# Inverting the triangular blocks of an RWKV-7 mixer on GpSimd instead of VectorE

## The chip, the cores and the metric

The kernel runs on one core of one Trainium2 chip. The metric is the device time of one execution in microseconds (us). Three runs of the kernel before took 2212.31, 2216.68 and 2216.26 us, median 2216.26 us.

## The reference

Two blocks follow each other on 256 tokens of width 2048. The second one has two mixers side by side, RWKV-7 (16 heads of 64 channels) and an attention with low-rank projections (MLA), then a projection and a feed-forward part. The change lies in the RWKV-7 mixer, whose core is a recurrence over tokens for each head:

```python
def rwkv7_scan(r, w, k, v, a, b):
    def step(state, inp):
        r_t, w_t, k_t, v_t, a_t, b_t = inp
        sa = jnp.einsum('bhvk,bhk->bhv', state, a_t)
        state = (state * w_t[:, :, None, :]
                 + sa[..., None] * b_t[:, :, None, :]
                 + v_t[..., None] * k_t[:, :, None, :])
        return state, jnp.einsum('bhvk,bhk->bhv', state, r_t)
    ...
```

The kernel doesn't step over tokens. It takes chunks of 64 tokens, and inside a chunk the term `sa` needs the inverse of a unit triangular 64x64 matrix. Of that matrix the kernel inverts the two 32x32 blocks on the diagonal by substitution and gets the rest with small matmuls.

## The kernel before, in words

Nearly all of the time goes into float32 matrix products whose weights are streamed from memory once. SP loads a piece of weights (`wraw`, 128 partitions x 1024 numbers). In `wsplit` ScalarE (ACT) casts it to a rounded half `whi` (L285), and VectorE (DVE) makes the rest, `wlo` = `wraw` - `whi` (L286). TensorE (PE) then needs both: in `lin` 24 matmuls for each piece at L327 to L329, two with `whi` and one with `wlo` for each product. `whi` and `wlo` have three buffers each, so ACT can be at most three pieces ahead of PE.

There are three phases. In phase b, `mixers` runs four groups G of four heads. For each group `rkv_lin` makes k, r and v (three large products), stores them with POOL's DMAs (`kdr`, L926), and `rwkv_prepare` loads them back (L938), forms the decays, and calls `tri_inverse` (L1044 on). `rwkv_chunks` then uses the inverse; it is called one group later, so that the group's chain of small steps runs beside the large products of the next groups and of the MLA part. The chain is long and each step is small: the products that fill PE meanwhile don't depend on it.

`tri_inverse` works as follows. DVE makes `Lc` from the masked blocks (L1051). ACT issues a DMA that stores it as `xd` (L1052) and eight DMAs that load it back (L1057, L1058) as `L`: each of the 32 blocks of a group lies along the free axis in all partitions that work on it. POOL issues the load of an identity into `T` (L1061). Then 31 steps follow, j = 0 to 30, each of two instructions: `tmp = l_j * t_j` (L1066, the tile `Tt` in the profile) and `T = T + tmp` (L1067). Both have 128 partitions and n x m numbers, n = j // 4 + 1, m = 31 - j, so from 8 to 76 numbers and 1560 in all for each line. Each instruction needs the one ahead of it. Last, ACT issues four DMAs that store `T` as `td` (L1069), one that loads it back in another layout as `Tc` (L1071), and DVE transposes `Tc` (L1072). `Lc`, `T` and `tmp` share the tag `tri` with two buffers, and `L` has one, so that one group's inversion must be over before the next one's begins.

Each engine runs its instructions in a fixed order, and so do the DMA issues in the queues of SP, ACT and POOL: an instruction that waits holds up what stands behind it on its engine. The order is made when the kernel is built, by a planner that plays the whole program through with costs of its own and takes, among what is ready, what has the highest priority: `rwkv_prepare` and `rwkv_chunks` are raised by `RP` = 6000, the weight pieces by `HP` = 1200. The planner's order is thus different when an instruction moves to another engine.

Of the kernel before, what the change touches and what calls it, by code (L numbers as in the profile page):

```python
# [12 lines left out]
ALU = mybir.AluOpType  # L13
# [103 lines left out]
class Kern:  # L117
# [926 lines left out]
    def tri_inverse(self, G, AB):  # L1044

        nc = self.nc
        xd = self.dr.tile([32, 32, 32], F32, tag=f"xd{G}", name=self.nm("xd"))
        td = self.dr.tile([32, 8, 4, 32], F32, tag=f"td{G}", name=self.nm("td"))
        small = lambda s, tag="tri": self.wk.tile([128, 8, 32], F32, tag=tag, name=self.nm(s))
        Lc = small("Lc")  # L1050
        nc.vector.tensor_tensor(Lc[:], AB[:, :, 0:32], AB[:, :, 32:64], ALU.add)  # L1051
        nc.scalar.dma_start(xd[:].rearrange("(c q) j i -> (q j) c i", q=4), Lc[:])  # L1052
        L = self.wk.tile([128, 768], F32, tag="L", bufs=1, name=self.nm("L"))
        L0, L1 = L[:, 0:512].rearrange("p (j i) -> p j i", i=32), L[:, 512:768].rearrange("p (j i) -> p j i", i=16)
        for q in range(4):
            qs = slice(32 * q, 32 * q + 32)
            nc.scalar.dma_start(L0[qs], xd[:, 0:16, :])  # L1057
            nc.scalar.dma_start(L1[qs], xd[:, 16:32, 16:32])  # L1058
        T, tmp = small("T"), small("Tt")
        o, n = CB["tinit"]  # L1060
        nc.gpsimd.dma_start(T[:], self.A["c_blk"][:, o : o + n].rearrange("p (c i) -> p c i", c=8))  # L1061
        for j in range(31):
            n, m = j // 4 + 1, 31 - j
            lj = (L0[:, j, j + 1 : 32] if j < 16 else L1[:, j - 16, j - 15 : 16]).unsqueeze(1).to_broadcast([128, n, m])
            tj = T[:, 0:n, j : j + 1].to_broadcast([128, n, m])
            nc.vector.tensor_tensor(tmp[:, 0:n, 0:m], lj, tj, ALU.mult)  # L1066
            nc.vector.tensor_tensor(T[:, 0:n, j + 1 : 32], T[:, 0:n, j + 1 : 32], tmp[:, 0:n, 0:m], ALU.add)  # L1067
        for q in range(4):
            nc.scalar.dma_start(td[:, :, q, :], T[32 * q : 32 * q + 32, :, :])  # L1069
        Tc, Tt = small("Tc", "trc"), small("Ttr", "trc")  # L1070
        nc.scalar.dma_start(Tc[:], td[:].rearrange("(c h) e q i -> (h e q) c i", h=4))  # L1071
        nc.vector.transpose(Tt[:], Tc[:])  # L1072
        return Tc, Tt
# [512 lines left out]
```

## Time and profile before

| what | value |
|---|---|
| median of 3 runs | 2216.26 us |
| the profiled execution: its time, its span | 2216.77 us, 2213.8 us |
| PE busy | 2168.2 us, 98% of the span |
| DVE busy | 1711.1 us, 77% |
| ACT busy | 1207.7 us, 55% |
| POOL busy | 106.4 us, 5% |
| mean granted TensorE clock | 0.995 of full speed |
| DMA traffic | 412.76 MB, mean 186 GB/s |

A busy share counts the time in which an engine has an instruction at work. PE's matmuls overlap each other, so the mean duration of one is longer than the distance between two. A PE that is busy all the time tells that the other engines are hidden behind it, whatever their share. The profile's time from the first to the last instruction is its span; about 3 us lie around it.

### The profile page before, as it was taken

The numbers are of one execution on the slowest core, as the hardware profiler recorded it, in microseconds if no ns is written. First come the engines' busy times: TensorE is split into PE (matmuls) and PEld (weight loads), VectorE is DVE, ScalarE is ACT, GpSimd is POOL, SyncE is SP. The second block draws the span as 40 slices with busy tenths as digits, with TensorE's granted clock in tenths as the row PEclk, the third lists the DMA queues.
The fourth block names the chain that finished last, engine by engine and source line by source line (L and its number), as shares of the span: only waits on it lengthen the run. The fifth ranks groups of instructions, "written<-read, shape, count | busy, mean of one in ns | idle before, by whom it ended". The sixth has DMA issues, their size and how long they took to land.

```text
span 2213.8 us, 36348 instructions
## 1 busy us (share of the span) xinstructions
PE 2168.2 (98%) x13687; PEld 1935.8 (87%) x13687; DVE 1711.1 (77%) x3176; ACT 1207.7 (55%) x1861; POOL 106.4 (5%) x253
## 2 busy tenths in 40 slices
PE   8999999999999999999999999999999999999997
PEld 7899988888899878899999888888888888888887
DVE  6999999778989889787787877776765576556765
ACT  6456636565566546665666556455443444444443
POOL 3100000000000000001100000020000000000000
PEclk9999999999999999999999999999999999999999
DMA  8875556666665457677774435476666666566654
GB/s 238 240 211 164 173 162 209 194 207 189 188 183 170 149 166 219 212 214 216 221 183 123 129 88 158 157 255 203 191 189 192 194 189 190 190 196 188 189 190 140
DMA packets 374511, 412.76 MB, mean 186 GB/s; under 512 B 40456, under 2 KB 327429, under 8 KB 373952
## 3 DMA queue, kind: packets, MB, share of 16 engines
q1 hardware_dynamic: 336464, 366.06, 54.4%
q0 software_dynamic: 10960, 31.79, 4.6%
q10 hardware_dynamic: 26912, 12.60, 2.4%
q8 instruction: 107, 1.75, 0.3%
q14 instruction: 68, 0.56, 0.1%
HBM read 390.47 MB, written 19.92 MB: 185 GB/s over the span
## 4 chain that ended last, share of the span: by engine, by line
PE 91%; DVE 3%; DMA 2%; ACT 2%; issue 1%; ACTq 1%; SPq 0%; DVEq 0%
PE wide L353 35%; PE wide L355 18%; PE lin L328 4%; PE lin L327 4%; PE lin L329 4%; PE lin L1401 3%; PE lin L1402 3%; PE lin L1400 3%; PE dn L1402 2%; PE dn L1401 2%; PE dn L1400 2%; PE po L709 1%; DVE wlo L286 1%; PE lin L1231 1%; PE lin L1232 1%; PE lin L1233 1%
## 5 line engine op out<-in xcount | busy, mean ns | idle before, releaser
L285 ACT CAST whi<-wraw 128x1024 fp32r<-128x1024 f32 (+1 forms) x708 | 725.2, 1027 | 670.6 <-PE wide L353 290.8
L286 DVE TENSOR_TENSOR wlo<-wraw,whi 128x1024 fp32r<-128x1024 f32 (+1 forms) x708 | 843.4, 1192 | 313.6 <-ACT whi L285 307.0
L353 PE MATMUL wide<-xs,whi 128*128 128x512 f32 x3492 | 853.0, 393 | 6.0 <-ACT whi L285 3.7
L353 PEld LDWEIGHTS wide<-xs,whi 128*128 128x128 f32 x3492 | 638.0, 189 | 129.8 <-ACT whi L285 5.3
L355 PEld LDWEIGHTS wide<-xs,wlo 128*128 128x128 f32 x3492 | 454.2, 191 | 25.8 <-DVE wlo L286 5.5
L355 PE MATMUL wide<-xs,wlo 128*128 128x256 f32 x3492 | 466.3, 284 | 3.6 <-DVE wlo L286 3.6
L327 PE MATMUL lin<-xs,whi 128*128 128x256 f32 x844 | 241.1, 286 | 1.2 <-ACT whi L285 0.6
L329 PE MATMUL lin<-xs,wlo 128*128 128x256 f32 x844 | 240.2, 285 | 1.6 <-DVE wlo L286 1.6
L328 PE MATMUL lin<-xs,whi 128*128 128x256 f32 x844 | 240.2, 285 | 0.0
L591 DVE SCALAR_TENSOR_TENSOR cy<-apad,vc_cw,cy 128x256 f32<-128x256 f32 x480 | 229.6, 480 | 6.7
L327 PEld LDWEIGHTS lin<-xs,whi 128*128 128x128 f32 x844 | 161.5, 191 | 2.7 <-ACT whi L285 0.8
L329 PEld LDWEIGHTS lin<-xs,wlo 128*128 128x128 f32 x844 | 161.5, 191 | 2.4 <-DVE wlo L286 1.8
L328 PEld LDWEIGHTS lin<-xs,whi 128*128 128x128 f32 x844 | 161.6, 191 | 1.1 <-issue 0.7
L1401 PE MATMUL lin<-wlo,xs 128*128 128x512 f32 (+1 forms) x304 | 117.4, 386 | 0.5 <-DVE wlo L286 0.5
L1402 PE MATMUL lin<-whi,xs 128*128 128x512 f32 (+1 forms) x304 | 117.0, 385 | 0.0
L1400 PE MATMUL lin<-whi,xs 128*128 128x512 f32 (+1 forms) x304 | 113.7, 386 | 1.2 <-ACT whi L285 1.2
L1400 PEld LDWEIGHTS lin<-whi,xs 128*128 128x128 f32 x304 | 57.1, 188 | 12.8 <-ACT whi L285 1.6
L1401 PEld LDWEIGHTS lin<-wlo,xs 128*128 128x128 f32 x304 | 57.2, 188 | 11.9 <-DVE wlo L286 1.0
L1400 PE MATMUL dn<-whi,xs 128*128 128x512 f32 (+1 forms) x176 | 67.0, 381 | 0.0
L1401 PE MATMUL dn<-wlo,xs 128*128 128x512 f32 (+1 forms) x176 | 67.0, 381 | 0.0
L1402 PE MATMUL dn<-whi,xs 128*128 128x512 f32 (+1 forms) x176 | 67.0, 381 | 0.0
L1402 PEld LDWEIGHTS lin<-whi,xs 128*128 128x128 f32 x304 | 57.1, 188 | 11.1
(544 smaller groups left out, 2401.1 us busy)
## 6 DMA issues: line engine op xcount, KB each, us to landing
wraw<-in_w_in_dram SPq DMA_DIRECT2D x244, 512.0 KB, 4.1
wraw<-in_w_out_dram SPq DMA_DIRECT2D x89, 512.0 KB, 4.0
wraw<-in_ffn_w_gate_dram SPq DMA_DIRECT2D x88, 512.0 KB, 4.1
wraw<-in_ffn_w_up_dram SPq DMA_DIRECT2D x88, 512.0 KB, 3.9
wraw<-in_ffn_w_down_dram SPq DMA_DIRECT2D x87, 512.0 KB, 4.3
wraw<-in_w_pg_dram SPq DMA_DIRECT2D x64, 512.0 KB, 4.5
bt<-btab POOLq DMA_DIRECT2D x32, 192.0 KB, 3.1
btab<-bF ACTq DMA_DIRECT2D x4, 1024.0 KB, 8.1
```

The lines of the kernel that those rows point to most:

```text
L285: nc.scalar.copy(hi[:], src)
L286: self.lo = nc.vector.tensor_tensor(lo[:], src, hi[:].bitcast(F32), ALU.subtract)
L327: nc.tensor.matmul(ps[:, t, :], lhsT=h, rhs=xh_, start=((t, k) == first), stop=False)
L328: nc.tensor.matmul(ps[:, t, :], lhsT=h, rhs=xl_, start=False, stop=False)
L329: nc.tensor.matmul(ps[:, t, :], lhsT=l, rhs=xh_, start=False, stop=((t, k) == last))
L353: nc.tensor.matmul(ps[t][:], lhsT=hi[:, i, ts], rhs=S.both(k).rearrange("p u c -> p (u c)"), **flags)
L355: nc.tensor.matmul(ps[t][:, :SEQ], lhsT=lo[:, i, ts], rhs=S.hi(k), **flags)
L591: prev, tail = tail, nc.vector.scalar_tensor_tensor(y, ap[:, t, k : k + SEQ], cw[:, k : k + 1], y, ALU.mult, ALU.add)
L709: nc.tensor.matmul(po[:, qb, g, :], lhsT=pT[:, kb, qb * 128 : qb * 128 + 128], rhs=vd[:, kb, j, :], start=(kb == 0), stop=(kb == 1))
L1400: nc.tensor.matmul(ps, lhsT=zh, rhs=hi, start=(k == 0), stop=False)
L1401: nc.tensor.matmul(ps, lhsT=zh, rhs=lo, start=False, stop=False)
L1402: nc.tensor.matmul(ps, lhsT=zl, rhs=hi, start=False, stop=(k == nt - 1))
```

## The change

The two instructions of each of the 31 steps are issued on POOL (GpSimd) instead of DVE. There are 4 groups, so 248 instructions move. Nothing else is written differently:

```diff
         for j in range(31):
             n, m = j // 4 + 1, 31 - j
             lj = (L0[:, j, j + 1 : 32] if j < 16 else L1[:, j - 16, j - 15 : 16]).unsqueeze(1).to_broadcast([128, n, m])
             tj = T[:, 0:n, j : j + 1].to_broadcast([128, n, m])
-            nc.vector.tensor_tensor(tmp[:, 0:n, 0:m], lj, tj, ALU.mult)
-            nc.vector.tensor_tensor(T[:, 0:n, j + 1 : 32], T[:, 0:n, j + 1 : 32], tmp[:, 0:n, 0:m], ALU.add)
+            nc.gpsimd.tensor_tensor(tmp[:, 0:n, 0:m], lj, tj, ALU.mult)
+            nc.gpsimd.tensor_tensor(T[:, 0:n, j + 1 : 32], T[:, 0:n, j + 1 : 32], tmp[:, 0:n, 0:m], ALU.add)
```

The planner's order moves with it. SP's queue stays as it is, and so does the order of the casts at L285. Three places matter.

The first is ACT's queue in group 0, where `td` (the stored inverse, from `T`) is issued among the casts. Numbers behind a name tell buffers apart. This is the difference, with + for the changed kernel:

```order
 L285 CAST whi_12885<-wraw_12799 128x1024
+L1069 DMA td_11033<-T_11046 256x1x32 x4
 L285 CAST whi_12927<-wraw_12919 128x1024
+L1015 COPY l_10501<-AR_11624 64x2x4x128 x2
 L285 CAST whi_12955<-wraw_12921 128x1024
+L1071 DMA Tc_11115<-td_11033 128x8x32
```

Before, the same issue stood six casts further on in that queue, as these rows of the kernel before show:

```order
L285 CAST whi_12927<-wraw_12919 128x1024
L285 CAST whi_12955<-wraw_12921 128x1024
L285 CAST whi_12983<-wraw_12923 128x1024
L404 ACTIVATE sq_12791<-lin_12792 128x512
L278 ACTIVATE cq_12789<-lin_12792,vc_c 128x256
L1015 COPY l_10501<-AR_11624 64x2x4x128 x2
L285 CAST whi_13011<-wraw_12925 128x1024
L984 COPY bd<-kk_11590 64x8x64 x2
L278 ACTIVATE cq_12789<-lin_12792,vc_c 128x256
L285 CAST whi_13087<-wraw_13079 128x1024
L285 CAST whi_13115<-wraw_13081 128x1024
L1069 DMA td_11033<-T_11046 256x1x32 x4
```

From the last DMA of `L` to the issue of `td` there are now 10, 6, 7 and 9 casts in the four groups; before there were 16, 11, 15 and 12.

The second place is POOL's queue in group 0, where the steps and the DMA issues that stood there before are now interleaved. In the changed kernel:

```order
L1066 TENSOR_TENSOR Tt_11047<-L_11037,T_11046 128x2x26
L1067 TENSOR_TENSOR T_11046<-T_11046,Tt_11047 128x2x26
L938 DMA v__1768_11561<-kdr_10271 128x512
L1066 TENSOR_TENSOR Tt_11047<-L_11037,T_11046 128x2x25
L926 DMA kdr_10272<-ko_12100 128x512
L761 MEMSET pp_12231 128x2
L1067 TENSOR_TENSOR T_11046<-T_11046,Tt_11047 128x2x25
L1066 TENSOR_TENSOR Tt_11047<-L_11037,T_11046 128x2x24
L1067 TENSOR_TENSOR T_11046<-T_11046,Tt_11047 128x2x24
L1066 TENSOR_TENSOR Tt_11047<-L_11037,T_11046 128x3x23
L938 DMA k__1766_11559<-kdr_10271 128x512
```

Between a group's first and last step POOL now issues 8, 4, 5 and 4 DMAs. Each step waits for the one ahead of it on POOL, and the issues stand in line with them.

The third place is DVE's queue, from which the steps are taken out; they stood between the `wlo` of the weight pieces:

```order
 L286 TENSOR_TENSOR wlo_12203<-wraw_12116,whi_12202 128x1024
-L1066 TENSOR_TENSOR Tt_11047<-L_11037,T_11046 128x30
-L1067 TENSOR_TENSOR T_11046<-T_11046,Tt_11047 128x30
-L1066 TENSOR_TENSOR Tt_11047<-L_11037,T_11046 128x29
 L286 TENSOR_TENSOR wlo_12249<-wraw_12240,whi_12248 128x1024
-L1067 TENSOR_TENSOR T_11046<-T_11046,Tt_11047 128x29
```

Besides, the load of the next group's identity (L1061) and the next group's `Lc` (L1051, on DVE) now wait for POOL, since their buffers are those of the steps, and an instruction that readies POOL for the new operation stands once in its queue, ahead of the first step.

## Rows read from the trace of the kernel before

**Rows 1.** The page: busy time, and the chain that ended last
```profile
PE 2168.2 (98%) x13687; PEld 1935.8 (87%) x13687; DVE 1711.1 (77%) x3176; ACT 1207.7 (55%) x1861; POOL 106.4 (5%) x253
...
PE 91%; DVE 3%; DMA 2%; ACT 2%; issue 1%; ACTq 1%; SPq 0%; DVEq 0%
```

**Rows 2.** Busy time by stretch: length, PE, PEld, DVE, ACT, POOL, granted clock, DMA
```profile
1090.00:1140.00 50.00, 50.00 (x410) 48.96 (x409) 44.36 (x118) 34.23 (x50) 4.78 (x12) 1.00 0.68 191
...
1200.00:1220.00 20.00, 18.24 (x196) 17.24 (x195) 9.88 (x23) 13.22 (x25) 1.22 (x3) 1.00 0.66 140
...
1260.00:1280.00 20.00, 16.93 (x147) 15.83 (x147) 14.61 (x49) 14.97 (x33) 0.54 (x1) 0.88 0.44 113
1280.00:1300.00 20.00, 18.54 (x160) 14.96 (x158) 14.60 (x46) 9.52 (x24) 2.17 (x4) 0.95 0.27 64
...
sum 255.00, PE 246.08 PEld 227.67 DVE 204.97 ACT 159.25 POOL 16.68; mean PE 24.61 PEld 22.77 DVE 20.50 ACT 15.93 POOL 1.67
```

**Rows 3.** Waits of PE from 1100 to 1350 us: total, times, longest
```profile
PE lin L329 <- DVE wlo L286: 1.6, 1, 1.6
PE pz L1090 <- DVE Ttr L1072: 1.2, 2, 0.8
```

**Rows 4.** Line L1066: duration in ns (min/median/max), first and last start
```profile
L1066 DVE TENSOR_TENSOR Tt<-L,T x124: 157/210/238, 1092.4 to 1336.0; 128x60 f32<-128x60 f32 x12, 128x28 f32<-128x28 f32 x8, 128x54 f32<-128x54 f32 x8, 128x48 f32<-128x48 f32 x8
```

**Rows 5.** DVE in order of time, group 0's first and last step: start, duration
```profile
1092.44 0.19 DVE L1066 TENSOR_TENSOR Tt<-L,T 128x31 f32<-128x31 f32 x1 [0.94 <-DMA L<-xd]
...
1138.25 0.17 DVE L1067 TENSOR_TENSOR T<-T,Tt 128x8 f32<-128x8 f32 x1
```

**Rows 6.** DVE's groups, 1092 to 1138 us: busy, mean ns, idle before
```profile
L286 DVE TENSOR_TENSOR wlo<-wraw,whi 128x1024 fp32r<-128x1024 f32 x15 | 18.3, 1221 | 1.7 <-ACT whi L285 1.4
L766 DVE SCALAR_TENSOR_TENSOR ko<-pp,vc_c,ko 128x256 f32<-128x256 f32 x6 | 2.6, 480 | 0.0
```

**Rows 7.** POOL's groups over the whole span: busy, mean ns, idle before
```profile
L926 POOL DMA_DIRECT2D kdr<-ko x12 | 6.6, 549 | 79.5 <-DVE Tt L1066 29.2 <-DVE ko L766 25.0 <-DVE T L1067 15.0
...
L495 POOL MEMSET apad<- 128x30 f32 x8 | 1.0, 134 | 142.6 <-DVE cy L591 142.6
...
L1186 POOL MEMSET bd<- 128x1024 f32 x1 | 1.0, 979 | 0.0
```

**Rows 8.** POOL in order of time: a fill, the fill that waits for it, a load
```profile
1014.33 0.98 POOL L1186 MEMSET bd<- 128x1024 f32 x1
1015.36 0.99 POOL L1188 MEMSET tx<- 32x512 f32 x2
...
1094.58 0.54 POOL L938 DMA_DIRECT2D v__1768_11561<-kdr  x1 [15.73 <-PE ptn L1027]
```

**Rows 9.** ACT and its queue (ACTq) in order of time: casts and `td` issues
```profile
1114.27 1.05 ACT L285 CAST whi<-wraw 128x1024 fp32r<-128x1024 f32 x1 [1.65 <-PE lin L328]
...
1120.07 1.05 ACT L285 CAST whi<-wraw 128x1024 fp32r<-128x1024 f32 x1 [1.06 <-issue]
...
1138.46 3.42 ACTq L1069 DMA_DIRECT2D td<-T  x4
...
1145.67 1.04 ACT L285 CAST whi<-wraw 128x1024 fp32r<-128x1024 f32 x1
...
1168.99 1.05 ACT L285 CAST whi<-wraw 128x1024 fp32r<-128x1024 f32 x1
...
1195.29 1.04 ACT L285 CAST whi<-wraw 128x1024 fp32r<-128x1024 f32 x1 [1.56 <-issue]
...
1206.55 1.05 ACT L285 CAST whi<-wraw 128x1024 fp32r<-128x1024 f32 x1
...
1221.09 1.05 ACT L285 CAST whi<-wraw 128x1024 fp32r<-128x1024 f32 x1 [1.82 <-issue]
...
1249.25 2.01 ACT L285 CAST whi<-wraw 128x1024 fp32r<-128x1024 f32 x2
...
1269.31 2.50 ACT L285 CAST whi<-wraw 128x1024 fp32r<-128x1024 f32 x3
```

## The prediction

> **What bounds the kernel now.** I read the page first, then the busy time by stretch, then the waits of PE, then the three queues that the change touches. On the page PE is busy for 98% of the span and makes 91% of the chain that ended last [rows 1]. The reader is to see there that DVE's 77% is hidden behind PE: a DVE instruction taken away is worth only the PE idle time that it causes. Where is that? The steps run from 1092.4 to 1336 us [rows 4], and in the 255 us from 1090 to 1345 PE is busy for 246.08 us [rows 2]. So 8.9 us of PE idle time is all there is to gain, and 6.3 of it lies in three of the stretches (1.76, 3.07 and 1.46 us), in which DVE is busy for 10 to 15 of 20 us, less than from 1090 to 1140, where PE never stops. Of the waits that name DVE the two longest lines come to 2.8 us [rows 3]. In two of these stretches the granted clock is 0.88 and 0.95 of full speed, which costs 0.12 x 20 + 0.05 x 20 = 3.4 us more. The bound of a gain is thus 8.9 + 3.4 = 12 us, and what DVE itself causes is nearer to 3.
>
> **What leaves DVE.** 248 instructions of about 0.21 us [rows 4], 52 us of DVE time in four stretches. PE hides it. It pays only through the waits above: I take 4 us as gained, bounds 0 and 12.
>
> **What POOL gets: the price of a step's instruction.** No POOL instruction of the trace reads SBUF, so the price is bounded. From below: a POOL fill of 128x30 takes 134 ns and one of 128x1024 takes 979 [rows 7], so a fill is 0.108 us + 0.85 ns for each number. A fill that waits for the one ahead of it begins 0.05 us after its end (1015.36 against 1014.33 + 0.98) [rows 8], and each of these instructions waits for the one ahead. A fill of the mean size, 50 numbers, would be 0.15 + 0.05 = 0.20 us. The instruction has three streams (two reads, one write) instead of one. If only the 0.85 ns counts three times, it is 0.108 + 0.128 + 0.05 = 0.29 us; if the fixed part does too, 0.50. The middle is 0.39. From above comes DVE's company. From 1090 to 1140 us DVE is busy for 44.36 of 50 us [rows 2], without the steps' 62 x 0.21 = 13 us for 31, and most of that reads two SBUF tensors: `wlo` alone is 18.3 us, 1.22 each, `ko` 2.6 [rows 6]. Call it 6 tenths of the time. If POOL and DVE had to take turns, a POOL instruction would meet one of these 6 times in 10 and wait half of it, near 0.5 us: 0.3 more each. I take a third of that, since ACT, once it stands still (below), gives DVE no `wlo` to make: 0.39 + 0.1 = **0.5 us**. It is also what POOL's only other busy row shows, 0.549 us for a DMA issue [rows 7]. Ends: 0.20 and 0.80.
>
> The rule that speaks against the change stands in the Trainium skill, "SBUF — State Buffer", section "Who interferes with whom": VectorE and GpSimd share a pair of ports under an exclusive lock, and a VectorE instruction with two SBUF inputs contends with a GpSimd one that reads SBUF. No row here shows it. By it the full 0.3 us would count; without it none.
>
> **The chain of a group.** 62 x 0.5 = 31.0 us, and the DMA issues that stand among the steps (8, 4, 5 and 4) at 0.55 us [rows 7]: 35.4, 33.2, 33.8 and 33.2 us. On DVE, among its other work, group 0 took 1092.44 to 1138.4, 46 us [rows 5]. So POOL's chain is shorter than DVE's, and that would be harmless if the rest stood where it did. It doesn't: the planner has moved what waits for the chain.
>
> **What waits for it.** `td` is issued by ACT, in line with the casts. It stood behind the last cast ahead of 1138.46 and now stands six casts earlier, behind the one that ran at 1120.07 [rows 9]. While ACT waits for POOL no weight piece is cast. I count the time that the new order leaves to the chain by the casts' old times. Group 0: `L` is there at 1092.44 [rows 5], ACT is at `td` at 1121.1: 28.7 us. Group 1: `td` stands behind the cast of 1168.99, and I count from the second cast behind the loads, at 1145.67 (the first one passes while they land): 24.4. Group 2: likewise from 1195.29 to 1222.1 (1221.09 and the cast's own 1.05), less about 5 for the old `td` issue and its waits that lie in between (no cast from 1195.29 to 1206.55): 22. Group 3: from 1250.3 (the second of the pair that begins at 1249.25) to the end of three casts at 1271.8: 21.5, taken as 22 [rows 9]. POOL is late by 35.4 - 28.7 = 6.7, then 9, 12 and 11 us, 39 in all.
>
> **What of it reaches PE.** Casts run 2.9 us apart (1114.27, then two casts on 1120.07), and three buffers are full when ACT stops, so PE lasts 8.6 us. The row before bears it out: from 1196.3 to 1206.55 ACT casts nothing, and 1200 to 1220 has only 1.76 us of PE idle time [rows 2, 9]. Of the 8.6 the four `td` issues themselves use 2.6 to 3.4 [rows 9], so 5.6 us of lateness is free in each group. What is left is 1.1 + 3.6 + 6.1 + 5.6 = 16 us of PE idle time. After 3.07 us of idle time the clock stood at 0.88 over 20 us [rows 2]; I add 4 us for that over the four places. DVE's own lateness by POOL (it would wait for a 0.5 us instruction now and then) is hidden by PE's 8.6 us.
>
> Other things that move: the load of k for the next group now stands behind 17 steps of this one, some 9 us later than before by 0.5 us each; it holds up ACT for a few us once in a group, inside the same 8.6 us, which fill again before `td` because a cast takes 1.05 of its 2.9 us. The v load waited 15.73 us for PE already [rows 8]. The instruction that readies POOL stands ahead of the first step, in that idle time, and costs nothing; without the cover it would be once. SP's queue doesn't change, and the stages from 1345 us on keep their order.
>
> **Sum.** + 16 + 4 - 4 = + 16 us against the profiled execution, 2213.8 us of span and 3 around it, 2216.8, which is 0.5 above the median. Forecast: **2233 us**, slower by 0.7%. A measurement can tell 0.2%, 4.4 us, from no change.
>
> **Rivals.**
> *The chain fits.* At 0.40 us an instruction or less the lateness is 31 - 24.8 = 6.2 us less in each group, 0.5, 3, 6 and 5, and all of it goes into the free 5.6. Then little is left but the small gain: 2213 to 2218 us, within 0.2%, likeliest 2215. For it: 0.39 without DVE's company; PE's 8.6 us of cover. Against it: 0.39 leaves out any waiting for DVE. Chance 0.2. The Trainium skill gives a figure that would lead here, "GPSIMD Engine Reference", section "Elementwise — side-by-side cycle accounting": 4497 ns for an addition of 2048 numbers in float32. By it 50 numbers are an estimated 0.11 us beside the fixed part, and the instruction would be near 0.27 us.
>
> *Faster.* This is decided below about 0.3 us: then the chain is 62 x 0.3 + 2.7 = 21 us instead of 46, it fits in every group, `td`, `Tc` and the chunk steps come early, and the gaps of 1200 to 1220 and 1260 to 1300 close: 1.76 + 3.07 + 1.46 = 6.3 us and 3.4 of clock, 9.7 in all, 2207 us. For it: PE's idle time sits just behind the `td` issues at 1198 and 1265 us. Against it: `td` and its DMAs keep their own time on ACT's queue. Chance 0.1.
>
> *POOL and DVE take turns in full.* At 0.69 us each group is 62 x 0.19 = 11.8 us later still, 47 in all, with some 5 of clock: 2285 us; at the end of 0.80 it is 18.6 x 4 = 74 and 10 more, 2317. For it: DVE's products of two SBUF tensors fill up to 6 tenths of the stretch [rows 2, 6]. Against it: ACT's stop starves DVE, and the rest of the chain is then undisturbed. Chance 0.2, most of it below 2285.
>
> **How the numbers follow.** The forecast's own case has 0.5. Slower is 0.5 + 0.2 = 0.7, within 0.2% is 0.2, faster 0.1. Both signs don't share the bulk, so one range does: from 2207, the faster rival, to 2285, where the third one has its middle; about 0.05 lies below and 0.15 above.
>
> **What would show it.** In the profile after: the L1066 and L1067 groups on POOL with the distance from one to the next near 0.5 us (a mean below 0.3 or above 0.7 makes the price wrong); the first to the last step of a group in 33 to 36 us; ACT idle ahead of `td` with POOL as the releaser, 7 to 12 us; PE waiting for `whi` behind it, 16 us in all, with a lower granted clock; DVE's busy time less by some 50 us. The forecast is wrong if `td` waits for nothing, or if PE idles in 1090 to 1345 us no more than the 8.9 us of before, or if the loss lies past 1345 us.

## The result, and the profile after

The changed kernel takes 2232.43 us (median of 4 runs, 2229.42 to 2234.07). The kernel before took 2215.79 us beside it (4 runs, 2212.31 to 2216.68). The ratio is 1.0076, with a 95% interval from 1.0059 to 1.0094: slower by 16.6 us. The forecast of 2233 us holds, and so does its sign. How the 16.6 us come about is another matter, and the profile shows it. The page of the changed kernel, busy time and the chain that ended last, to be read against [rows 1]:

```profile
PE 2179.7 (98%) x13687; PEld 1947.5 (87%) x13687; DVE 1680.5 (75%) x2928; ACT 1207.8 (54%) x1861; POOL 206.1 (9%) x501
...
PE 88%; DVE 3%; POOL 3%; DMA 2%; ACT 2%; issue 1%; ACTq 1%; SPq 0%; POOLq 0%; DVEq 0%
```

PE still has 13687 matmuls, yet it is busy for 11.5 us longer (2168.2 before). Its idle time is span less busy time: 2231.8 - 2179.7 = 52.1 us against 2213.8 - 2168.2 = 45.6, so 6.5 us more. The two make the 18.0 us by which the two profiled spans differ. Two thirds of the loss is thus not idle time: the same matmuls run slower, and the granted clock is lower (a mean of 0.988 against 0.995). This sum, busy and idle, is the first thing to do with such a page. POOL has come into the chain with 3%.

Where it lies: the busy time by stretch, of the kernel before and then of the changed one (length, PE, PEld, DVE, ACT, POOL, granted clock, DMA share, GB/s).

```profile
1080.00:1200.00 120.00, 118.74 (x1027) 114.01 (x1025) 99.73 (x291) 76.76 (x127) 7.55 (x18) 1.00 0.62 166
1200.00:1400.00 200.00, 190.86 (x1581) 169.38 (x1580) 150.92 (x444) 117.43 (x255) 12.11 (x24) 0.98 0.44 127
```

```profile
1080.00:1200.00 120.00, 112.08 (x891) 106.54 (x890) 72.05 (x137) 67.76 (x114) 62.05 (x143) 0.91 0.52 139
1200.00:1400.00 200.00, 189.51 (x1600) 170.68 (x1600) 136.38 (x343) 118.47 (x260) 57.16 (x147) 0.97 0.44 125
...
1090.00:1140.00 50.00, 43.43 (x321) 41.69 (x321) 29.67 (x49) 27.86 (x41) 32.49 (x75) 0.92 0.56 157
1200.00:1220.00 20.00, 17.29 (x182) 16.61 (x182) 13.08 (x25) 14.45 (x28) 0.00 (x0) 0.91 0.46 119
1260.00:1280.00 20.00, 18.33 (x200) 17.44 (x199) 13.37 (x27) 13.25 (x28) 1.78 (x4) 1.00 0.34 99
1280.00:1300.00 20.00, 18.29 (x157) 16.80 (x156) 15.82 (x40) 9.88 (x22) 8.96 (x23) 1.00 0.65 160
1130.00:1140.00 10.00, 5.88 (x34) 5.39 (x33) 3.50 (x4) 5.44 (x7) 1.69 (x6) 0.78 0.46 108
1140.00:1150.00 10.00, 10.00 (x108) 9.54 (x108) 4.15 (x7) 7.11 (x16) 0.00 (x0) 0.71 0.50 130
1180.00:1190.00 10.00, 9.97 (x62) 9.50 (x60) 9.64 (x28) 5.63 (x10) 8.98 (x14) 0.66 0.35 105
```

From 1080 to 1200 us, with groups 0 and 1, PE does 891 matmuls where it did 1027, is idle for 7.9 us (1.3 before) and has 0.91 of the clock (1.00 before). Behind 1200 us there is about as much of both as before. The last three rows show a lower clock beside and behind idle time: PE is idle for 4.1 of 10 us at 0.78, and in the next 10 us, without idle time, it has 0.71; from 1180 to 1190, behind 1.3 us of idle time, it is busy nearly throughout at 0.66, a mean between its two levels of 1.2 and 2.4 GHz. Not every idle stretch does this: from 1260 to 1300 us PE is idle for 3.4 us and keeps 1.00.

POOL's groups over the whole inversion, against [rows 4] for the duration on DVE, and the line's own view:

```profile
L1066 POOL TENSOR_TENSOR Tt<-L,T 128x60 f32<-128x60 f32 (+24 forms) x124 | 50.2, 405 | 72.4 <-DMA L<-xd 63.6
L1067 POOL TENSOR_TENSOR T<-T,Tt 128x60 f32<-128x60 f32 (+24 forms) x124 | 49.4, 398 | 9.2
...
L1066 POOL TENSOR_TENSOR Tt<-L,T x124: 209/299/1357, 1090.7 to 1319.9; 128x60 f32<-128x60 f32 x12, 128x28 f32<-128x28 f32 x8, 128x54 f32<-128x54 f32 x8, 128x48 f32<-128x48 f32 x8
```

The median is 299 ns and the longest of this line 1357 (of L1067, 2216): a few are held up, and most are not. Group 0's steps take from 1090.67 to 1131.76 us, 41.1 us; groups 1 to 3 take 33.9, 34.7 and 29.3 us. On DVE the steps took 46.0, 44.9, 50.9 and 40.4 us, and they ended 6.7, 5.7, 6.1 and 16.3 us later than on POOL. So the inverse is there earlier in every group, and the kernel is slower all the same: POOL is late only against the new order, which puts the reader of `T` earlier still. Added up over the 248 instructions, 139.0 us are these: the shortest duration of each shape 68.9 us, the hops from one to the next 17.8, what 34 instructions of over 0.6 us (13, 10, 6 and 5 in the four groups) and some lesser ones have beyond their shortest 30.7, and the DMA issues in POOL's queue with their waits 21.6. What holds them up stands on DVE at the same time. POOL in order of time, then DVE (start, duration):

```profile
1116.22 1.32 POOL L1066 TENSOR_TENSOR Tt<-L,T 128x66 f32<-128x66 f32 x1
...
1118.90 1.28 POOL L1067 TENSOR_TENSOR T<-T,Tt 128x60 f32<-128x60 f32 x1
```

```profile
1116.16 1.21 DVE L286 TENSOR_TENSOR wlo<-wraw,whi 128x1024 fp32r<-128x1024 f32 x1
...
1118.80 1.23 DVE L286 TENSOR_TENSOR wlo<-wraw,whi 128x1024 fp32r<-128x1024 f32 x1
```

Of the 34 long ones 22 end 0.08 to 0.18 us behind a `wlo`, and most of the others behind another DVE instruction that reads two SBUF tensors. It goes the other way too, but little: seven `wlo` that begin while a step is running take 1.26 to 1.32 us, where none of the kernel before takes over 1.23. And this is where ACT stood still, in order of time, first for group 0 and then for the other three (ACTq is its DMA issue):

```profile
1105.24 0.91 ACT L971 ACTIVATE kk<-k__1766_11559,vc_c 128x256 f32<-128x256 f32 x2 [4.00 <-DMA k__1766_11559<-kdr]
...
1122.82 1.05 ACT L285 CAST whi<-wraw 128x1024 fp32r<-128x1024 f32 x1 [0.66 <-ACT ko L765]
1131.79 2.56 ACTq L1069 DMA_DIRECT2D td<-T  x4
1134.47 1.04 ACT L285 CAST whi<-wraw 128x1024 fp32r<-128x1024 f32 x1 [10.60 <-issue]
...
1175.35 0.91 ACT L971 ACTIVATE kk<-k__1882_12369,vc_c 128x256 f32<-128x256 f32 x2 [3.39 <-DMA k__1882_12369<-kdr]
...
1192.58 2.54 ACTq L1069 DMA_DIRECT2D td<-T  x4
1195.23 1.05 ACT L285 CAST whi<-wraw 128x1024 fp32r<-128x1024 f32 x1 [3.96 <-DMA td<-T]
...
1202.19 1.65 ACT L1095 COPY tx<-Tc 32x256 f32<-32x256 f32 x4 [2.96 <-DMA Tc<-td]
...
1259.20 2.56 ACTq L1069 DMA_DIRECT2D td<-T  x4
1261.82 0.91 ACT L765 ACTIVATE ko<-pp,omu 128x256 f32<-128x256 f32 x2 [5.31 <-issue]
...
1320.48 2.57 ACTq L1069 DMA_DIRECT2D td<-T  x4
1323.09 0.37 ACT L1338 COPY mla<-mo 128x256 f32<-128x256 f32 x1 [5.07 <-DMA td<-T]
```

The waits behind `td` include the 2.5 us of its own issues. Without them ACT stood still for POOL for 7.9 us in group 0 (from the end of the cast at 1122.82 to 1131.79) and for some 1.3, 2.7 and 2.5 us in the others. But there is a second place, `kk` at L971: it needs the load of k for the next group, which stands among steps in POOL's queue. The first two of these loads begin right behind a step; the third, at 1243.30 us, begins 0.5 us after the store that it reads has landed (1242.77), so that its wait (2.3 us) isn't for the steps alone. A third place is ACT's copies of `Tc`, at 1202.19 us. PE's longest waits of 1080 to 1360 us (total, times, longest), against [rows 3]:

```profile
PE pch L1122 <- ACT Y L1119: 4.5, 3, 2.7
PE ss L905 <- ACT sq L972: 4.1, 3, 2.5
PE lin L327 <- ACT whi L285: 3.6, 1, 3.6
```

`ss` waits for `sq`, which ACT makes behind `kk`; `lin` waits for the cast behind `td` of group 0; the longest wait of `pch`, 2.7 us at 1205.70, stands behind ACT's copies of `Tc`.

### The profile page after: what moved, and what is told of

It is laid out like the page before. It is cut to its first block, busy times and chain, and to the rows that moved or that the text cites. A ratio compares the mean times of both kernels' runs of the same rounds, so it can differ in the third digit from the quotient of the medians.

```text
span 2231.8 us, 36344 instructions
## 1 busy us (share of the span) xinstructions
PE 2179.7 (98%) x13687; PEld 1947.5 (87%) x13687; DVE 1680.5 (75%) x2928; ACT 1207.8 (54%) x1861; POOL 206.1 (9%) x501
## 4 chain that ended last, share of the span: by engine, by line
PE 88%; DVE 3%; POOL 3%; DMA 2%; ACT 2%; issue 1%; ACTq 1%; SPq 0%; POOLq 0%; DVEq 0%
PE wide L353 35%; PE wide L355 18%; PE lin L329 4%; PE lin L328 4%; PE lin L327 4%; PE lin L1401 3%; PE lin L1402 3%; PE lin L1400 3%; PE dn L1402 2%; PE dn L1401 2%; PE dn L1400 2%; POOL T L1067 1%; POOL Tt L1066 1%; PE po L709 1%; DVE wlo L286 1%
## 5 line engine op out<-in xcount | busy, mean ns | idle before, releaser
L285 ACT CAST whi<-wraw 128x1024 fp32r<-128x1024 f32 (+1 forms) x708 | 724.8, 1027 | 674.3 <-PE wide L353 292.7
L327 PE MATMUL lin<-xs,whi 128*128 128x256 f32 x844 | 244.6, 290 | 4.9 <-ACT whi L285 4.3
L328 PE MATMUL lin<-xs,whi 128*128 128x256 f32 x844 | 244.0, 289 | 0.0
L327 PEld LDWEIGHTS lin<-xs,whi 128*128 128x128 f32 x844 | 164.9, 195 | 6.5 <-ACT whi L285 4.7
L328 PEld LDWEIGHTS lin<-xs,whi 128*128 128x128 f32 x844 | 164.9, 195 | 1.1 <-issue 0.7
```

The source lines that it names most:

```text
L285: nc.scalar.copy(hi[:], src)
L327: nc.tensor.matmul(ps[:, t, :], lhsT=h, rhs=xh_, start=((t, k) == first), stop=False)
L328: nc.tensor.matmul(ps[:, t, :], lhsT=h, rhs=xl_, start=False, stop=False)
```

## The experiments

The first theory, A: the chain on POOL is late for the place that the order gives it, because DVE's instructions with two SBUF inputs hold POOL's up, and ACT stands still behind it. Against it stands that the price of POOL's instruction and the queue that it stands in cost this by themselves. C, D and E came up on the way; what each letter expects of a run stands there.

**The price of a step by itself.** A small kernel that computes nothing of the block and writes zeros: the 62 instructions on POOL alone, and then four times more, each time with 24 or 48 DVE instructions of one kind issued beside them.

```diff
+    for kind in range(4):
+        chain()
+        for _ in range(24):
+            if kind == 0:
+                nc.vector.tensor_tensor(lo[:], a[:], b[:], ALU.subtract)
...
+            else:
+                nc.vector.tensor_scalar(lo[:], a[:], 2.0, None, ALU.mult)
```

> A kernel by itself: it leaves out the whole computation and writes zeros. GpSimd runs the 62 instructions of one group's chain five times: alone; beside VectorE subtracting two SBUF tensors of 128x1024 (as wlo does); beside VectorE subtracting with one operand in PSUM; beside VectorE reductions of one SBUF tensor; beside VectorE scaling one SBUF tensor. Theory A (the two engines take turns where VectorE reads two SBUF tensors, and that is what stretched the chain in the changed kernel): 0.35 us an instruction, 21 to 23 us a chain, alone, beside the PSUM form and beside the reductions; beside the two-tensor subtraction 35 us or more, with single GpSimd instructions of 1.0 to 1.5 us. Rival B (the long instructions of the changed kernel come from something else, such as DMA traffic or GpSimd's own DMA issues): all five chains within 10%.

Measured: 22.1 us alone, 0.36 us for each instruction, with a median duration of 0.28. Beside the two-input subtraction it is 44.0 us; beside the one that reads PSUM 22.1, beside reductions (of which only 7 overlapped it) 22.1. The last chain, meant for the one with one SBUF input, took 23.3. POOL and DVE in order of time, beside the two-input subtraction:

```profile
31.50 1.30 POOL L41 TENSOR_TENSOR T<-T,tmp 128x31 f32<-128x31 f32 x1
32.88 1.17 POOL L40 TENSOR_TENSOR tmp<-L,T 128x30 f32<-128x30 f32 x1
34.13 1.18 POOL L41 TENSOR_TENSOR T<-T,tmp 128x30 f32<-128x30 f32 x1
```

```profile
31.47 11.30 DVE L57 TENSOR_TENSOR wlo<-wraw,whi 128x1024 f32<-128x1024 f32 x9
```

As long as DVE runs such instructions back to back, POOL gets one instruction through for each of them (1.25 us apart; 11.30 / 9 = 1.26), and DVE isn't slowed at all: its 24 have a mean of 1226 ns, against 1221 in [rows 6]. So the company is real. By the Trainium skill, "SBUF — State Buffer", section "Who interferes with whom", VectorE and GpSimd share one pair of ports and the loser is fully blocked; this run agrees, with POOL as the loser. In the changed kernel a `wlo` that met a running step was delayed too, by 0.1 us at most.

The 23.3 us are no price of an instruction with one SBUF input: DVE was at the reductions until 148.60 us, so that the chain ran beside these until then (none of its steps was held), and only its last three steps ran beside the one-input scaling. All three were held, for 0.57 to 0.65 us in place of some 0.22. The first and the last of them, then DVE:

```profile
149.04 0.57 POOL L41 TENSOR_TENSOR T<-T,tmp 128x16 f32<-128x16 f32 x1
...
150.40 0.65 POOL L41 TENSOR_TENSOR T<-T,tmp 128x8 f32<-128x8 f32 x1
```

```profile
148.83 2.15 DVE L64 TENSOR_SCALAR wlo<-wraw 128x1024 f32<-128x1024 f32 x3
```

So this kind of instruction holds POOL's up as well, for its own 0.69 us instead of 1.22. This bears on the runs below that were to be without DVE's company.

**The two places, one at a time and together.** One edit moves `td` and `Tc` off ACT's queue, the other the loads of k, r and v off POOL's:

```diff
-            nc.scalar.dma_start(td[:, :, q, :], T[32 * q : 32 * q + 32, :, :])
+            nc.gpsimd.dma_start(td[:, :, q, :], T[32 * q : 32 * q + 32, :, :])
...
-        nc.scalar.dma_start(Tc[:], td[:].rearrange("(c h) e q i -> (h e q) c i", h=4))
+        nc.gpsimd.dma_start(Tc[:], td[:].rearrange("(c h) e q i -> (h e q) c i", h=4))
```

```diff
-            nc.gpsimd.dma_start(t[:], self.kdr[G][:, u])
+            nc.sync.dma_start(t[:], self.kdr[G][:, u])
```

> The changed kernel, with the store of T (td, L1069) and the load back (Tc, L1071) issued by GpSimd behind the steps instead of by ScalarE. ScalarE then first meets the chain at the copies of Tc (L1095), 14, 9, 10 and 12 casts behind the loads of L instead of 10, 6, 7 and 9. Theory A (ScalarE stood still at td because the chain came later than the order allowed): the 4 to 11 us stops of ScalarE at td are gone or much shorter, TensorE idles less, about 2222 us (2217 to 2227). Rival B (the loss is made by the new order as a whole, or by VectorE and GpSimd sharing, and not by this wait): 2230 us or more.

> The changed kernel, with the loads of k, r and v (L938) issued by SP, so that the k load no longer stands behind the steps in GpSimd's queue; td stays on ScalarE. Theory A (the k load behind 17 or more steps is a second stop of ScalarE, 4.0, 3.4 and 2.3 us at L971): these waits vanish, the stops at td stay, about 2227 us (2222 to 2231). Rival B (only the stop at td counts, the buffers cover the other): no change, 2232 us. Rival C (SP's queue is held up by these loads and the weights come late): 2235 us or more.

> Both edits together: td and Tc on GpSimd's queue, the loads of k, r and v on SP's. Theory A (two places at which ScalarE waits for GpSimd make the loss): near the kernel before, 2217 us (2212 to 2222). Rival B (order as a whole, or the sharing of VectorE and GpSimd): still 2228 us or more.

Measured: `td` moved 2226.65 us (ratio to before 1.0053, interval 1.0038 to 1.0068), k moved 2231.99 (1.0075, 1.0058 to 1.0092), both 2222.0 (1.0029, 1.0016 to 1.0041). The first and the last are at the upper end of what A gave them. With k alone moved nothing is won, as the rival B had it and not A (2222 to 2231 us): the waits of ACT from 1080 to 1360 us show that its stop has gone to `td`. A wait of 3.3 us at `kk` is left, for the third load.

```profile
ACT whi L285 <- DMA td<-T: 12.5, 2, 8.4
ACT whi L285 <- issue: 11.1, 1, 11.1
```

With both moved no wait for `td` is left, and the stop is at the next place that needs the chain, ACT's copies of `Tc` and PE's products behind them:

```profile
ACT tx L1095 <- DMA Tc<-td: 19.3, 4, 8.0
...
PE pz L1090 <- DVE Ttr L1072: 6.3, 1, 6.3
```

With both places moved 10.4 of the 16.6 us are gone; the chains in that run are about as long as in the changed kernel (38.1, 37.0, 31.7 and 29.6 us). What of this is the two stops and what the new order, this run can't tell; the same moves on DVE's steps come below.

**With less of DVE's company.** If A is right, taking away the two-input instructions gives the loss back. From the first group's products to the last group's (the MLA inputs among them) the low half becomes `whi` times a constant, so this part of the weights is left out; the same edit on the kernel before is the base.

```diff
-        self.lo = nc.vector.tensor_tensor(lo[:], src, hi[:].bitcast(F32), ALU.subtract)
+        self.lo = nc.vector.tensor_scalar(lo[:], hi[:].bitcast(F32), 2.0**-12, None, ALU.mult) if getattr(self, 'one', 0) else nc.vector.tensor_tensor(lo[:], src, hi[:].bitcast(F32), ALU.subtract)
```

> While the groups' products run, the low half of each weight piece is no longer wraw - whi but whi times a constant, so that DVE's instruction (L286) has one SBUF input instead of two; the low half of these weights is left out of the result. The steps stay on POOL. Theory A (an instruction of the steps is held for about 1 us whenever DVE runs one with two SBUF inputs): at most 3 instructions of a group take over 0.6 us (13, 9, 6 and 5 in the changed kernel), the chains of groups 1 to 3 fall from 34, 35 and 29 us to 23 to 28, group 0's from 41 to 28 to 34 (its DMA issues stay), ACT's waits at td shrink to under 4 us each, and the time is within 6 us of the same kernel with the steps on DVE (the next run). Theory B (the price of a POOL instruction and the queue that it stands in are the whole of it, DVE's company doesn't matter): chains as in the changed kernel within 2 us, and 12 to 18 us slower than the next run.

> The kernel before with the same low half from one SBUF input: the base for the run ahead of it. DVE has about 0.5 us less for each of some 100 pieces, which PE hides: both theories expect the time of the kernel before, 2208 to 2217 us. What counts is the difference of the two runs: theory A at most 6 us, theory B 12 to 18.

Measured: 2229.56 us (1.0065, 1.0046 to 1.0084) and 2212.11 us (0.9983, 0.9973 to 0.9994), a difference of 17.4 us, as B had it and not A (at most 6). But B's chains, within 2 us of the changed kernel's, didn't come true either, and the edit did less than A's test needs. The company did shrink, if less than expected:

```profile
L1066 POOL TENSOR_TENSOR Tt<-L,T x124: 211/298/843, 1083.4 to 1320.2; 128x60 f32<-128x60 f32 x12, 128x28 f32<-128x28 f32 x8, 128x54 f32<-128x54 f32 x8, 128x48 f32<-128x48 f32 x8
```

The longest of L1066 is 843 ns instead of 1357, all that is beyond the shortest 19.9 us instead of 30.7, and the chains are 36.3, 28.9, 28.7 and 26.5 us. But 31 instructions still take over 0.6 us (11, 7, 7 and 6 in the groups, where A's test asked for at most 3), and 14 of them end just behind the one-input `wlo`. POOL and DVE in order of time:

```profile
1113.97 0.75 POOL L1067 TENSOR_TENSOR T<-T,Tt 128x42 f32<-128x42 f32 x1
```

```profile
1113.91 0.68 DVE L286 TENSOR_SCALAR wlo<-whi 128x1024 fp32r<-128x1024 f32 x1
```

As in the small kernel, the one-input instruction holds a step up for the rest of its 0.69 us. The edit makes the company shorter, and doesn't take it away. The chains are 3 to 6 us shorter in each group, and it is worth nothing: the edit gains the changed kernel 2.9 us and the kernel before 3.7. ACT's stops for POOL are still there, at k in three groups and at `td`:

```profile
ACT mla L1305 <- DMA td<-T: 7.0, 1, 7.0
...
ACT kk L971 <- DMA k__1766_11559<-kdr: 5.5, 1, 5.5
ACT bd L984 <- issue: 5.2, 1, 5.2
ACT kk L971 <- DMA k__2072_13753<-kdr: 4.9, 1, 4.9
```

The planner's order moved with the edit (9, 7, 6 and 6 casts ahead of `td` instead of 10, 6, 7 and 9), so this pair says only that shorter chains alone don't mend it. How much of the loss DVE's company makes stays open, since no run of the block is without it.

**Half of the groups.** `eng` is GpSimd for two groups and VectorE for the others (the second run has `G >= 2`), in both instructions of a step:

```diff
+        eng = nc.gpsimd if G < 2 else nc.vector
...
-            nc.gpsimd.tensor_tensor(tmp[:, 0:n, 0:m], lj, tj, ALU.mult)
+            eng.tensor_tensor(tmp[:, 0:n, 0:m], lj, tj, ALU.mult)
...
```

> The steps of groups 0 and 1 on POOL, those of groups 2 and 3 on DVE. Theory A (each group is late on its own, by its chain's length against the order's place for td): the loss splits by group. PE idle and clock in the changed kernel lie about as much before 1205 us (groups 0 and 1) as behind it, so 2222 to 2228 us here, and this loss and that of the next run add up to 16 us within 4. Theory C (one place makes the loss: group 0, whose chain is the longest with its 8 DMA issues, and the stop that follows from it): 2229 to 2234 here, and the next run within 3 us of the kernel before.

> The steps of groups 2 and 3 on POOL, those of groups 0 and 1 on DVE. Theory A: 2221 to 2227 us, waits of ACT at td in groups 2 and 3 as in the changed kernel and none in groups 0 and 1. Theory C: 2214 to 2219 us.

Measured: groups 0 and 1 alone 2232.71 us (1.0081, 1.0063 to 1.0100), the whole loss; groups 2 and 3 alone 2223.0 us (1.0032, 1.0018 to 1.0046). 17.7 and 8.0 make 25.7, not 16: the losses don't add up. C had the first number right and the second one wrong, A the second right, and its sum, that each group is late on its own, wrong. What groups 2 and 3 cost by themselves is mainly one stop, at `td` of group 2, and what it does to the clock. The edit adds a line, so `td` is L1070 here. ACT and PE in order of time, and the stretch, of the second run:

```profile
1245.64 2.56 ACTq L1070 DMA_DIRECT2D td<-T  x4
1248.25 0.91 ACT L971 ACTIVATE kk<-k__2072_13753,vc_c 128x256 f32<-128x256 f32 x2 [10.03 <-issue]
...
1252.61 1.02 PE L905 MATMUL ss<-cblk,sq 128*128 128x2 f32 x4 [5.61 <-ACT sq L972]
...
1240.00:1280.00 40.00, 33.48 (x225) 30.76 (x226) 22.59 (x58) 20.16 (x40) 8.18 (x22) 0.74 0.38 107
```

ACT waits 7.4 us for POOL and 2.6 more for its issues, with `kk` of the next group behind them; PE is idle for 6.5 of 40 us and has 0.74 of the clock. In the changed kernel ACT waited for POOL for 2.7 us at this `td`. There groups 0 and 1 had delayed everything by then; that this is why their company makes it cheaper was not tested.

**Both places moved, with less of the company; and the same moves on DVE's steps.** The edits are those above, in combination.

> Steps on POOL with both places moved (td and Tc issued by POOL, the load of k by SP) and the low half of the groups' weights from one SBUF input (so left out of the result). Theory D (the loss comes from the places where ACT stands still, at k, at td and then at Tc; a POOL instruction that is held by DVE only makes the last of these longer): with k and td gone and the chains at 24 to 30 us, ACT's waits at the copies of Tc are at most 4 us each, and the time is within 4 us of the next run. Theory E (steps on POOL cost some 6 us in any order, since k, td and Tc were not all of it): 6 us or more above the next run.

> The same with the steps on DVE: the base for the run ahead of it. 2208 to 2216 us; only the difference of the two tells the theories apart (D: at most 4 us, E: 6 or more).

> The kernel before, steps on DVE, with the two places moved alone: td and Tc issued by POOL, the load of k by SP. It says how much of what the two moves gave back on POOL's steps (16.6 us of loss down to some 6) they would give to the kernel before as well. Theory D: ACT hardly waited at these places before, so within 4 us of the kernel before, 2212 to 2220 us, and the moves mend what the change broke. The other reading (they are worth as much to any kernel): 2204 to 2208 us.

> The kernel before, steps on DVE, with td and Tc issued by POOL and nothing else moved: the control of the run in which this edit gave the changed kernel some 6 us back, and a candidate for a kernel faster than both. Reading 1 (the edit mends a stop that POOL's chain causes; DVE's chain was not late for td, for which ACT hardly waited): 2212 to 2219 us, as the kernel before. Reading 2 (an issue of td off ACT's queue frees about 3 us of ACT in each group, which any kernel gains): 2204 to 2210 us.

Measured: 2218.9 us (1.0010, 1.0002 to 1.0019), its base 2203.45 (0.9940, 0.9927 to 0.9952); DVE's steps with both places moved 2219.07 (1.0014, 1.0004 to 1.0023), with `td` and `Tc` moved alone 2221.33 (1.0024, 1.0014 to 1.0035). The third came out as D had it; the base of 2203.45 lies below its range of 2208 to 2216, and the last one missed both readings: the move that gains the changed kernel some 6 us costs the kernel before 5. All in one table (busy and idle are PE's, of the one profiled execution, which lies up to 4 us off its kernel's median; us):

| steps | `td`, `Tc` | k | low half | median | PE busy | PE idle |
|---|---|---|---|---|---|---|
| DVE | ACT | POOL | 2 inputs | 2215.8 | 2168.2 | 45.6 |
| POOL | ACT | POOL | 2 inputs | 2232.4 | 2179.7 | 52.1 |
| POOL | POOL | POOL | 2 inputs | 2226.7 | 2176.4 | 48.8 |
| DVE | POOL | POOL | 2 inputs | 2221.3 | 2174.9 | 44.4 |
| POOL | ACT | SP | 2 inputs | 2232.0 | 2179.5 | 52.0 |
| POOL | POOL | SP | 2 inputs | 2222.0 | 2170.0 | 46.1 |
| DVE | POOL | SP | 2 inputs | 2219.1 | 2175.2 | 43.0 |
| POOL | ACT | POOL | 1 input | 2229.6 | 2178.4 | 53.3 |
| DVE | ACT | POOL | 1 input | 2212.1 | 2169.5 | 38.7 |
| POOL | POOL | SP | 1 input | 2218.9 | 2170.9 | 46.5 |
| DVE | POOL | SP | 1 input | 2203.5 | 2166.3 | 35.9 |

What follows. On POOL's steps the two moves are worth the same twice: 2232.4 - 2222.0 = 10.4 us, and with one input 2229.6 - 2218.9 = 10.7. On DVE's steps the same moves cost 3.3 us in one pair and gain 8.7 in the other, though ACT hardly waited for k or `td` there: that is most likely the planner's order falling out another way, and its size, several us of either sign, is the limit of what these pairs can tell. Beyond what they do on DVE's steps the moves are thus worth 13.7 us in one pair and 2.0 in the other: the stops at k and `td` stand in the traces, but how much of the loss they carry isn't shown. With both places moved POOL's steps cost 0.15% (1.0029 against 1.0014, a difference that the intervals don't separate from none) with two inputs, but 15.5 us with one. The second pair was the test of D against E, and E holds there; the first pair is what D would give. In the second POOL's kernel still waits for `Tc` (ACT 14.2 us in three places, PE behind it 6.9 in two) and DVE's doesn't:

```profile
ACT tx L1095 <- DMA Tc<-td: 14.2, 3, 6.9
...
PE pz L1090 <- DVE Ttr L1072: 6.9, 2, 3.8
```

It isn't that POOL's chains are longer: they take 32.0, 31.2, 28.7 and 28.5 us in this pair, DVE's 33.1, 35.2, 38.3 and 39.5. But from the loads of `L` to ACT's first copy of `Tc` the order leaves 12, 9, 8 and 13 casts with POOL's steps, and 14, 10, 11 and 18 with DVE's. How much of these 15.5 us is that wait, and how much a lucky order of the base, stays open: a run that keeps one order and changes the durations alone was not tried, as the order is remade with every edit. None of the kernels that compute the whole block is faster than the kernel before.

## Why the prediction was right or wrong

**Right: the mechanism's outline.** `td` was the longest single stop, ahead of it the queue's casts stood still, PE ran out of `whi` behind it (3.65 us at 1135.57), the clock fell, DVE's relief was hidden, and the stages behind 1400 us are as before: PE is idle for 14.8 us from there to the end in both (817.0 of 831.8 us busy; before 799.0 of 813.8). That POOL's chain would be shorter than DVE's, and the loss come from the place of `td` in the order, was said and came true.

**The price of an instruction** was put at 0.5 us on POOL, 0.39 of it undisturbed. The small kernel shows 0.36 undisturbed, with 2.1 ns for each number ((1799 - 318) / (768 - 64), from its instructions of 768 and 64 numbers) where a fill takes 0.85: the streams count about two and a half times. DVE's company adds 30.7 / 248 = 0.12, put at 0.1, so "a third of 0.3" was near, though the "6 tenths of the time" behind it took all of DVE's other 31 us for work with two SBUF inputs, of which the two lines named make 20.9. The figure of the Trainium skill's "GPSIMD Engine Reference", section "Elementwise — side-by-side cycle accounting" (4497 ns for 2048 numbers, 2.2 ns each), agrees with the 2.1 ns for each number. The rival's 0.27 us came out at 0.36 undisturbed, since the fixed part is 0.18 us (318 ns less 64 x 2.1) and the hop 0.08 where the fills show 0.108 and 0.05. Its conclusion, that the chain then fits, failed for these and for DVE's company and the DMA issues beside the instructions.

**The chains** came out at 41.1, 33.9, 34.7 and 29.3 us where 35.4, 33.2, 33.8 and 33.2 were said. Group 0 is longer by the DMA issues: 8 at 0.55 us were counted, 4.4 us, and they took 9.5 with what they wait for; the last one, a store of `ko`, came 2.40 us late.

**The lateness failed as a size.** 6.7, 9, 12 and 11 us were said, 39 in all; ACT stood still at `td` for 7.9, 1.3, 2.7 and 2.5, 14.4 in all. The step that failed is the time that the order leaves, which was counted from the casts' old times: 28.7, 24.4, 22 and 22 us were said, and from a group's first step to ACT's arrival at `td` it was 33.2, 32.6, 32.0 and 26.9. ACT itself reached `td` later. In group 0 it had stood 4.0 us at k; that elsewhere PE, at a lower clock, gave the `whi` buffers back later is likely, but not shown.

**The k load failed as a step.** It was said to be 9 us later and inside the 8.6 us of cover. It is issued at 1101.64 instead of 1098.57 us, 3.1 later; but ACT then stands at `kk` for 4.0, 3.4 and 2.3 us, and PE waits 4.1 us for `ss`. The cover of three `whi` buffers holds for `lin` alone: `ss` stands in PE's own queue ahead of the next products, and full buffers don't help it.

**The split of the sum failed; the sum held.** Said were 16 of PE idle time, 4 of clock and a gain of 4; measured are 6.5 of idle time, net, and 11.5 of longer busy time. The clock term had one row of 20 us at 0.88 behind it [rows 2], 2.4 us, which at each of four places would be 9.6 and was put at 4; in fact 120 us ran at 0.91, which is 10.8. That the two errors cancel is luck. Of what was named as a sign, the distance of 0.5 us (0.56 measured, 0.47 without the DMA issues), the lower clock and the loss ahead of 1400 us came true; 16 us of PE waiting for `whi` did not (3.6), nor did 50 us less for DVE: the page has 30.6 less, though the two lines' own sums, 25.6 and 25.5, are gone. Their records overlapped others, which the page's busy time counts once.

**The rivals.** POOL and DVE do take turns in full, beside back-to-back instructions; in the kernel 34 of 248 are hit, and the rival's 0.69 us isn't reached. DVE's relief shows no gain in sum: in the three stretches of before PE idles for 2.71, 1.67 and 1.71 us after 1.76, 3.07 and 1.46. The clock is 1.00 from 1260 to 1300 us, where it was 0.88 and 0.95, but 0.91 from 1200 to 1220, where it was 1.00; other work lies in these stretches now.

## What to carry to other kernels

When work moves to an idle engine, look first at what reads its result from an in-order queue, and at what else stands in the queue it moves into: here the chain on the new engine was shorter and ended earlier, and the kernel still lost, with stops at a store that reads the result from ACT's queue and at a load that stands among the steps in POOL's. Taking both out of the way gave 10 of 16.6 us back, though part of that may be the new order. Split a loss on PE into idle time and longer busy time at once: here idle time was 6.5 us of it and longer busy time, at a lower clock, 11.5. And where every edit remakes the order, give each experiment its own base with the other side of the change, since the same two moves were worth -3 to +9 us where hardly anything waited for them.

## What the runs showed of the hardware

- A GpSimd instruction that reads SBUF is held for the rest of a VectorE instruction with two SBUF inputs: 62 of them take 44.0 us instead of 22.1, VectorE's stay at 1226 ns. In the whole kernel a VectorE instruction that meets a running GpSimd one is delayed by up to 0.1 us (1.32 us where it takes 1.22). Beside a VectorE instruction with one SBUF and one PSUM input nothing is held (22.1 us).
- A VectorE `tensor_scalar` with one input, from SBUF to SBUF in float32, holds it as well: the three GpSimd instructions that met one took 0.57 to 0.65 us instead of some 0.22, and in a whole kernel (there with fp32r output) 14 of over 0.6 us end just behind one. Beside VectorE reductions of one SBUF tensor nothing is held (58 steps of one chain).
- A small two-input float32 instruction on GpSimd takes 0.21 to 0.35 us for 8 to 76 numbers and the next one that needs it begins 0.08 us after its end; on VectorE it took 0.16 to 0.24 [rows 4]. For work this small the slower engine isn't far behind.
- The granted clock can be lower in the 10 us behind a stretch of idle time, with PE busy all the time: 0.71 behind 4.1 us of idle time. It need not be: 1.00 from 1270 to 1280 us, behind 1.7 us.
